# Rearranging the joints of a two-layer decoder step: up phases begun pair by pair, block sums moved, two norm banks, groups held over a phase border

## The chip, the cores and the metric

The kernel runs on all 8 cores of one Trainium2 chip. Each core holds one eighth of the batch (one prompt sequence of 2048 positions and 16 decode tokens, 2064 columns in all) and all weights pass through each core; the cores do not talk to each other. The metric is the device time in microseconds (us) of the slowest core.

The program has a second, slower state. In some executions the cores of one die, sometimes of both, show a lower granted TensorE clock and the whole is some per cent longer: in a run of the kernel before of 1492.06 us the cores of one die took 1473.2 to 1490.5 us at a mean clock of 0.837 to 0.852, those of the other 1317.0 to 1322.5 us at 0.977 to 0.980; both dies were lower in a run of 1513.85 us (0.822 to 0.826 and 0.942 to 0.945).

Engine names: PE is TensorE (matmuls), DVE is VectorE, ACT is ScalarE, POOL or Pool is GpSimd. PEld is the weight load of PE, which overlaps its matmuls (PE is busy 1270.9 and PEld 808.9 us in one span of 1338.7, below).

## The reference, cut to what matters

Layer 0 has a pooling mixer and a gated convolution, layer 1 a chunked gating mixer. Both end in an output projection, a residual addition, an RMSNorm and a SwiGLU feed-forward block.

```python
for layer in range(DEPTH):                       # DEPTH = 2
    h = rmsnorm(x, norm_mix[layer])
    if layer % 2 == 0:
        z = h @ w_in_even[e]                     # the "first projection" below
        ...                                      # pooling windows 2/4/8/16, short convolution
        mix = jnp.concatenate([a_out, b_out], axis=-1) @ w_out_even[e]   # "even out projection"
    else:
        z = jax.nn.gelu(h @ w_in_odd[o], approximate=False)              # "v" and "u" phases
        c_out, v = chunk_gating(z, norm_sg[o], w_s[o], b_s[o])
        mix = c_out @ w_out_odd[o]               # "odd out projection"
    x = x + mix
    h = rmsnorm(x, norm_ffn[layer])
    x = x + swiglu(h, ffn_w_gate[layer], ffn_w_up[layer], ffn_w_down[layer])
return rmsnorm(x, norm_final), ...

def rmsnorm(x, g):
    y = xf * lax.rsqrt(jnp.mean(xf * xf, axis=-1, keepdims=True) + EPS)
    return (y * g).astype(x.dtype)

def swiglu(h, w_gate, w_up, w_down):             # 1024 -> 2816 -> 1024
    return (jax.nn.silu(h @ w_gate) * (h @ w_up)) @ w_down
```

## The kernel before

Activations lie with features on partitions and tokens along the free dimension. The 2064 tokens form 6 tiles of 344 columns, and two neighbouring tiles form a pair. Features form 8 groups of 128.

The feed-forward block is cut into 22 chunks of 128 hidden features. They are taken in three rounds per layer; a round is an *up phase* (gate and up products of 6 or 8 chunks) and a *down phase* (the projection back of these chunks into the residual). An up product of one chunk and one pair of tiles uses the seven-multiplication scheme for a 2x2 block product: 7 x 4 = 28 matmuls of 344 columns instead of 32. The price is block sums: sums of weight blocks (`ssum`, four per chunk, into `S`) and sums of activation blocks (`tsum`, four per pair, into `T`; one of them rewrites a part of `hT` in place).

```python
FFN_GROUPS = ((8, 8, 6), (6, 8, 8))

NB = banks[7]                                   # one PSUM bank for every norm

class Norm:
    POPS = (2, 1, 1, 0, 1, 1, 1, 1)
    def square(self, n, c):                     # squares on ACT, their running sum on Pool
        ...
        act(rng[i][:], xs(c, n), AF.Square)
        dst = accb[a] if c == lastc else acc[a]
        tt("pool", dst[:], acc[a][:], rng[i][:], ALU.add)
    def mid(self, n):                           # sum over partitions on PE, then 1/sqrt on ACT
        for i, p_ in enumerate(ps):
            sc.op("pe", lambda E, i=i, p_=p_: E.matmul(
                NB[:, 0:TW], lhsT=ones[:], rhs=p_[:], start=(i == 0), stop=(i == len(ps) - 1)))
        rsqrt_mean(NB, NB[:, 0:TW])
        self.q += [(n, c) for c in range(KC)]   # eight scalings to do on DVE: hT = x * g * NB
        if self.sums and n % 2:
            self.q += [("T", n // 2, i) for i in range(4)]     # the block sums of the pair
    def before(self, n, m):
        if m == 4 and n > 0:
            self.mid(n - 1)
...
def tsum(p, i):                                 # block sums of the activations
    if i == 0:   tt("dve", T1, b12, b11, ALU.subtract)
    elif i == 1: tt("pool", b12, b22, b12, ALU.subtract)       # rewrites hT
    elif i == 2: tt("dve", T2, b22, T1, ALU.subtract)
    else:        tt("dve", T4, b21, T2, ALU.subtract)
...
def out_proj(l, slots, nm):
    todo = [(c, i) for c in (0, 1) for i in range(4)]
    for n in range(NT):                         # 6 tiles
        for m in range(8):                      # 8 output groups of 128 features
            nm.before(n, m)
            bk = nbank()
            proj(bk, slots[m // 4], (m % 4) * 128, n, mix, 512)   # 8 matmuls
            xacc(bk, m, n)                      # residual addition on DVE
            nm.step(n, m)                       # squares, scalings, block sums
            if n >= 2 and m in (2, 6) and todo:
                ssum(l, *todo.pop(0), eng="pool")              # weight sums on Pool
...
def ffn_up(l, g):
    order = [(c, p) for c in range(c0, c1) for p in range(NPAIR)]
    if g == 0:
        order[0:6] = [(0, 0), (0, 1), (1, 0), (1, 1), (0, 2), (1, 2)]
    ...
    for i in range(len(gs) + 2):                # software pipeline over products cur, prv, pp
        if cur:
            cur.pe(1); cur.pe(7); cur.c1(); cur.c7()
        if pp:
            pp.mb(dst(pp))
        if prv:
            prv.pe(5); prv.pe(2); prv.d1(); prv.ga(); prv.ma(dst(prv))
        if cur:
            cur.pe(6); cur.c2()
            if i == 0 and active and g == 0 and active[0].parts:
                drip(len(active[0].q))
                active[0].mid(NT - 1)           # norm of the last tile, inside the up phase
            cur.pe(4); cur.d2()
        ...
...
def ffn(l, nm, before_last=None):
    for g in range(3):
        ffn_up(l, g)
        ...
        ffn_dn(l, g, nm if g == 2 else None)
...
def n_sq(n, cs=range(KC)):                      # squares of the first projection
    ...
        who = (("act", "dve")[c % 2] if n == 0 else ("act", "dve", "pool")[c % 3] if n < 3 else
               ("act", "act", "pool")[c % 3] if n < 4 else ("act", "pool")[c % 2])
```

Cuts are marked with `...`; some lines were joined or left out. In the profile, `L433`, `L436` and `L430` are the helpers behind every DVE or Pool `tensor_tensor`, every DVE `scalar_tensor_tensor` and every ACT operation, so there one goes by tile names: `xTs` is the residual, `hTs` its normed copy, `tmp` the buffers of the up products, `acc` and `accb` the running sums of squares. `L554` is the norm-sum matmul, `L659` an up product, `L703` a projection, `L809` a down projection, `L901` the pooling part of the first projection.

## Time and profile before

| | before |
|---|---|
| time, median of 6 runs | 1326.03 us (1321.43 to 1444.6) |
| profiled execution, slowest core (core 7, at clock 0.81 for 158.4 us) | 1338.7 us |
| profiled execution, core 2 (undisturbed) | 1319.1 us |
| matmuls | 8200 |

The page of the profile first: busy time and instructions of each engine on the slowest core, then the busy share of PE and the granted clock in 40 equal slices (tenths), then the chain of waits that ended last.

```profile
PE 1270.9 (95%) x8200; PEld 808.9 (60%) x8200; DVE 827.7 (62%) x1621; ACT 539.4 (40%) x1157; POOL 268.6 (20%) x343
...
PE   8799999699999999999889999888999999999996
...
PEclk9988887899999999999999999888999999999999
...
PE 82%; DVE 10%; issue 4%; ACT 2%; POOL 1%; DMA 1%; DVEq 0%; POOLq 0%; ACTq 0%; SPq 0%
```

What PE waits for stands in the view of its waits. This is core 2, before; the columns are the releaser, us in total, times, and the longest wait in us.

```profile
PE bank L554 <- DVE hTs L436: 16.9, 9, 3.7
PE bank L659 <- DVE tmp_107 L433: 12.1, 8, 3.8
PE bank L659 <- ACT bank L430: 9.1, 5, 4.3
PE bank L901 <- DVE hTs L436: 7.9, 3, 4.7
...
PE bank L554 <- POOL accb_92 L433: 3.2, 3, 1.9
```

The first line is the norm-sum matmul. It writes bank 7, and DVE's eight scalings of the tile before still read bank 7. The waits of up products (`L659`) on `tmp_107` and on ACT are DVE and ACT behind in the first products of an up phase.

These lines are PE's timeline on core 2 in the even out projection (start, duration, instruction, count, and in brackets the idle time before it with what ended it).

```profile
190.65 4.83 PE L703 MATMUL bank<-mix,wring_48 128*128 128x344 f16 x32
...
199.16 0.31 PE L554 MATMUL bank<-accb_92,ones 128*128 128x344 bf16 x1 [3.68 <-DVE hTs L436]
199.30 6.50 PE L703 MATMUL bank<-mix,wring_46 128*128 128x344 f16 x32
```

The same 32 matmuls take 4.83 us before a wait of 3.68 us and 6.50 us after it. In the clock record of this core the clock is 1.00 up to 199.71 us, 0.50 for the next 3.41 us, and 1.00 again. The up phase that follows shows the half clock more strongly. These are windows of 3 us on core 2: length, then busy us with instruction counts of PE, PEld, DVE, ACT, POOL, then granted clock, DMA share and GB/s.

```profile
218.00:221.00 3.00, 0.00 (x0) 0.00 (x0) 3.00 (x6) 0.85 (x3) 2.80 (x4) 0.87 0.00 0
221.00:224.00 3.00, 1.30 (x4) 0.44 (x4) 3.00 (x10) 0.88 (x2) 1.50 (x2) 0.50 0.27 31
224.00:227.00 3.00, 1.98 (x8) 1.07 (x9) 0.76 (x2) 0.96 (x2) 1.31 (x2) 0.50 0.34 61
227.00:230.00 3.00, 3.00 (x12) 1.65 (x11) 2.93 (x6) 0.90 (x2) 0.90 (x1) 0.50 0.00 0
```

For the first three of these us PE does nothing, DVE is full and Pool is busy beside it; by the clock record the clock is 0.50 from 220.19 to 230.43 us. At 0.50 matmuls of 344 columns start every 0.286 us (226.69 to 230.13), at full clock every 0.146 (next paragraphs). In the first projection there is another kind of loss. This is core 2's timeline of DVE and Pool there, some lines of it.

```profile
59.52 4.28 DVE L436 SCALAR_TENSOR_TENSOR mix<-P_70,Sg_88 128x344 f16<-128x344 f32 x1
59.79 0.78 POOL L433 TENSOR_TENSOR mix<-P_67 128x344 f16<-128x344 f32 x1
60.51 0.77 POOL L433 TENSOR_TENSOR sq_77<-xTs 128x344 bf16<-128x344 f32 x1
...
62.66 0.75 POOL L433 TENSOR_TENSOR sq_83<-xTs 128x344 bf16<-128x344 f32 x1
```

One pooling instruction of DVE takes 4.28 us while Pool runs a row of its own instructions. In the same trace such an instruction took 0.52 us with Pool idle (at 65.11 us, for one) and 0.81 to 0.82 us beside one or two of Pool's (at 46.09, 49.15 and 73.53 us).

### The profile page before, as it was taken

How to read it: one execution, taken by the hardware profiler on the slowest of the kernel's cores; microseconds unless marked ns; L12 is line 12 of the kernel's file. 1: busy time of each engine (PE TensorE's matmuls, PEld its weight loads, DVE VectorE, ACT ScalarE, POOL GpSimd, SP SyncE). 2: the span in 40 equal slices, each digit the busy share in tenths (PEclk: the TensorE clock that was granted, in tenths of full speed). 3: DMA queues.
4: the chain of work that ended last, by engine and by line, in shares of the span. 5: the costliest groups of instructions: out<-in, count | busy, mean ns of one | idle time of the engine just before them, and what ended most of it. 6: DMA issues, size and time to landing. Idle time of an engine off the chain costs nothing.

```text
span 1338.7 us, 25276 instructions; the slowest of 8 cores (1314.7 to 1338.7 us)
## 1 busy us (share of the span) xinstructions
PE 1270.9 (95%) x8200; PEld 808.9 (60%) x8200; DVE 827.7 (62%) x1621; ACT 539.4 (40%) x1157; POOL 268.6 (20%) x343
## 2 busy tenths in 40 slices
PE   8799999699999999999889999888999999999996
PEld 4466665366666666666544566555666666666664
DVE  3878557856545665455765676885665665456566
ACT  3332333355204550055557434344503551055543
POOL 4300057500000000000641103761000000000054
PEclk9988887899999999999999999888999999999999
DMA  9442230063101620042333103003311421034024
GB/s 240 119 67 33 33 49 1 9 95 64 33 1 33 96 48 16 1 64 33 64 64 63 35 1 49 1 1 65 63 17 33 92 51 18 1 64 79 2 89 167
DMA packets 18913, 68.64 MB, mean 51 GB/s; under 512 B 2928, under 2 KB 3056, under 8 KB 17744
## 3 DMA queue, kind: packets, MB, share of 16 engines
q0 software_dynamic: 13472, 54.99, 23.4%
q1 hardware_dynamic: 4736, 11.26, 2.5%
q8 instruction: 69, 1.13, 0.3%
q10 hardware_dynamic: 576, 0.77, 0.2%
q14 instruction: 60, 0.49, 0.1%
HBM read 105.84 MB, written 9.18 MB: 86 GB/s over the span
## 4 chain that ended last, share of the span: by engine, by line
PE 82%; DVE 10%; issue 4%; ACT 2%; POOL 1%; DMA 1%; DVEq 0%; POOLq 0%; ACTq 0%; SPq 0%
PE bank L659 38%; PE bank L809 18%; PE bank L703 14%; PE bank L1101 4%; PE bank L1067 4%; DVE hTs L436 2%; DVE xTs L433 2%; PE bank L901 2%; DVE mix L433 1%; DVE xTs L436 1%; DMA xTs<-xT 1%; DVE T_98 L433 1%; PE bank L554 1%; PE bank L1114 1%; PE bank L890 1%
## 5 line engine op out<-in xcount | busy, mean ns | idle before, releaser
L433 DVE TENSOR_TENSOR xTs<-bank,xTs 128x344 f32<-128x344 f32 x384 | 197.1, 515 | 169.7 <-PE bank L809 132.4
L809 PE MATMUL bank<-mix,wring_46 128*128 128x344 f16 x1152 | 215.0, 309 | 0.0
L809 PE MATMUL bank<-mix,wring_48 128*128 128x344 f16 x960 | 187.0, 309 | 0.0
L430 ACT ACTIVATE bank<-bank 128x344 f32<-128x344 f32 x161 | 71.2, 442 | 227.6 <-DVE xTs L433 210.3
L809 PEld LDWEIGHTS bank<-mix,wring_46 128*128 128x128 f16 x1152 | 112.5, 98 | 54.9
L809 PEld LDWEIGHTS bank<-mix,wring_48 128*128 128x128 f16 x960 | 93.9, 98 | 46.1
L430 ACT ACTIVATE tmp_111<-bank 128x344 f32<-128x344 f32 x132 | 60.4, 458 | 119.1 <-DVE tmp_108 L433 43.3
L659 PE MATMUL bank<-hTs,raw_102 128*128 128x344 f16 x576 | 103.2, 316 | 0.0
L436 DVE SCALAR_TENSOR_TENSOR hTs<-xTs,vecs_s,bank 128x344 f16<-128x344 f32 x184 | 97.9, 565 | 7.5 <-ACT bank L430 7.1
L430 ACT ACTIVATE tmp_110<-bank 128x344 f32<-128x344 f32 x132 | 60.4, 457 | 100.5 <-DVE tmp_106 L433 31.6
L659 PE MATMUL bank<-hTs,raw_103 128*128 128x344 f16 x504 | 87.6, 310 | 0.0
L659 PE MATMUL bank<-hTs,raw_104 128*128 128x344 f16 x504 | 87.4, 309 | 0.2 <-DVE xTs L433 0.2
L659 PEld LDWEIGHTS bank<-hTs,raw_102 128*128 128x128 f16 x576 | 57.6, 100 | 30.1 <-issue 0.3
L703 PE MATMUL bank<-mix,wring_48 128*128 128x344 f16 x384 | 66.5, 338 | 0.0
L181 POOL DMA_DIRECT2D raw_102<-wts x16 | 8.6, 538 | 286.3 <-DVE tmp_107 L433 166.6
L430 ACT ACTIVATE rng_94<-xTs 128x344 bf16<-128x344 f32 x82 | 40.2, 490 | 63.5 <-DVE xTs L433 56.1
L433 DVE TENSOR_TENSOR mix<-tmp_110,tmp_109 128x344 f16<-128x344 f32 x66 | 38.5, 583 | 44.0 <-ACT tmp_110 L430 44.0
L703 PE MATMUL bank<-mix,wring_46 128*128 128x344 f16 x384 | 65.0, 333 | 0.0
L659 PEld LDWEIGHTS bank<-hTs,raw_103 128*128 128x128 f16 x504 | 49.5, 98 | 24.5
L659 PEld LDWEIGHTS bank<-hTs,raw_104 128*128 128x128 f16 x504 | 49.2, 98 | 24.6 <-issue 0.5
L433 DVE TENSOR_TENSOR mix<-tmp_110,tmp_108 128x344 f16<-128x344 f32 x66 | 34.1, 517 | 47.1 <-ACT tmp_110 L430 47.1
L430 ACT ACTIVATE rng_93<-xTs 128x344 bf16<-128x344 f32 x82 | 40.2, 490 | 57.2 <-DVE xTs L433 54.4
(262 smaller groups left out, 2208.5 us busy)
## 6 DMA issues: line engine op xcount, KB each, us to landing
raw_102<-wts POOLq DMA_DIRECT2D x16, 512.0 KB, 6.2
yT<-xTs SPq DMA_DIRECT2D x22, 344.0 KB, 2.3
raw_103<-wts POOLq DMA_DIRECT2D x14, 512.0 KB, 6.2
raw_104<-wts POOLq DMA_DIRECT2D x14, 512.0 KB, 6.3
xTs<-xT POOLq DMA_DIRECT2D x10, 688.0 KB, 17.4
wring_46<-wts POOLq DMA_DIRECT2D x12, 512.0 KB, 9.2
wring_48<-wts POOLq DMA_DIRECT2D x10, 512.0 KB, 8.4
wring_48<-wts POOLq DMA_DIRECT2D x2, 1024.0 KB, 16.9
```

The costliest lines, as they stand in the source:

```text
L430: return sc.op("act", lambda E: E.activation(out=out, in_=in_, func=func, **k))
L433: return sc.op(eng, lambda E: E.tensor_tensor(out=out, in0=in0, in1=in1, op=op))
L436: return sc.op("dve", lambda E: E.scalar_tensor_tensor(out=out, in0=in0, scalar=scalar, in1=in1, op0=op0, op1=op1))
L554: sc.op("pe", lambda E, i=i, p_=p_: E.matmul(NB[:, 0:TW], lhsT=ones[:], rhs=p_[:], start=(i == 0), stop=(i == len(ps) - 1)))
L659: last = E.matmul(bk[:, 0:TW], lhsT=w_[:, o_ + k * 128:o_ + (k + 1) * 128], rhs=rhs(k), start=(first and k == 0), stop=(k == 3), skip_grou ...
L703: last = E.matmul(bk[:, 0:TW], lhsT=wt[:, o:o + 128], rhs=src[:, k, tok(n)], start=(k == 0), stop=(k == KC - 1))
L809: last = E.matmul(bk[:, 0:TW], lhsT=w_(jl)[:, m * 128:(m + 1) * 128], rhs=mix[:, jl, tok(n)], start=(jl == 0), stop=(jl == n_ - 1))
L890: sc.op("pe", lambda E: E.matmul(bk[:, 0:512], lhsT=ones[:], rhs=spinw[:], start=True, stop=True))
L901: last = E.matmul(pdst[n][g][:, 0:TW], lhsT=wt0[:, k * 512 + g * 128:k * 512 + (g + 1) * 128], rhs=hT[:, k, tok(n)], start=(k == 0), stop= ...
L1067: last = E.matmul(bk[0:ntok, :], lhsT=hT[:, k, t0:t0 + ntok], rhs=wv[:, k * 512:(k + 1) * 512], start=(k == 0), stop=(k == KC - 1))
L1101: last = E.matmul(bu[:, 0:w], lhsT=wt[:, o:o + 128], rhs=hT[:, k, c0:c0 + w], start=(k == 0), stop=(k == KC - 1))
L1114: last = E.matmul(bm[:, q * 128:(q + 1) * 128], lhsT=vN[:, q0 + q, h * 128:(h + 1) * 128], rhs=wsT[:, h * 128:(h + 1) * 128], start=True, ...
```

## The change

The intent is to take the waits of PE out of the joints between phases without changing the mathematics or the number of matmuls:

1. The first five chunks of the first up phase of a layer run pair by pair, so that the phase begins with products of tiles 0 and 1 and reaches tiles 4 and 5 only after ten products. The last norm and the block sums of pairs 1 and 2 move behind these products. Five slots for weights and weight sums replace three.
2. The block sums of pairs 1 and 2 leave the projection phases; the weight sums and the rewriting `tsum` go from Pool to DVE.
3. Norms alternate between two banks, each output group is followed by one scaling, and the norm sum comes one group later.
4. The last group of an out projection or of a down phase is held and issued inside the next up phase; the first group of a down phase is pulled into the end of its up phase.
5. In the first projection the squares of tiles 2 to 5 all go to ACT, and one pooling task runs per tile, interleaved with the convolution; three of the pooling tasks move to the even out projection.
6. The chunks of layer 0 are grouped 6, 8, 8 instead of 8, 8, 6.

```diff
-FFN_GROUPS = ((8, 8, 6), (6, 8, 8))
+FFN_GROUPS = ((6, 8, 8), (6, 8, 8))
...
-        NB = banks[7]
+        def NB(n):
+            return banks[7 if n % 2 else 2]
...
             def step(self, n, m):
                 self.square(n, m)
-                k_ = self.POPS[m]
-                if self.sums and n % 2 and n > 1 and m in (3, 4, 5, 6):
-                    self.pop_sum()
-                self.pop_h(k_)
+                if n < NT - 1 or m < 5 or self.late:
+                    self.pop(1)
 
             def before(self, n, m):
-                if m == 4 and n > 0:
+                if m == 5 and n > 0:
                     self.mid(n - 1)
...
             elif i == 1:
-                tt("pool", b12, b22, b12, ALU.subtract)
+                tt("dve", b12, b22, b12, ALU.subtract)
...
-                    if n >= 2 and m in (2, 6) and todo:
-                        ssum(l, *todo.pop(0), eng="pool")
+                    if (n, m) == (NT - 1, KC - 1):
+                        held.append(lambda bk, n=n, m=m: group(n, m, bk))
+                    else:
+                        group(n, m)
+                    ...
+                    if tasks:
+                        tasks.pop(0)()
+                    elif todo and (n > 0 or m > 3):
+                        ssum(l, *todo.pop(0))
+                    if (n, m) in tsums:
+                        tsum(0, tsums[(n, m)])
...
             if g == 0:
-                order[0:6] = [(0, 0), (0, 1), (1, 0), (1, 1), (0, 2), (1, 2)]
+                order = [(c, p) for p in range(NPAIR) for c in range(5)] + order[15:]
...
+                early = {0: [lambda: nm.pop(4)], 1: [lambda: nm.pop(4)], 2: ss(3), 3: ss(4) + ts(1, 0), 4: ts(1, 1, 2, 3),
+                         5: [lambda: nm.pop(4)], 6: [lambda: nm.pop(4)], 7: ts(2, 0, 1), 8: ts(2, 2, 3)}
...
+                    release(banks[(ctr[0] - len(gs) + 2) % 3 if g else 6])   # the held group
+                    if g == 0 and i == 1:
+                        nm.mid(NT - 1)
...
-                who = (("act", "dve")[c % 2] if n == 0 else ("act", "dve", "pool")[c % 3] if n < 3 else
-                       ("act", "act", "pool")[c % 3] if n < 4 else ("act", "pool")[c % 2])
+                who = ("act", "dve")[c % 2] if n == 0 else ("act", "dve", "pool")[c % 3] if n == 1 else "act"
```

Cuts are marked. Not shown: the new places of buffers (for the five slots and for the split weights of the v phase), SiLU done in place in its PSUM bank, the interleaving of pooling and convolution tasks, and the order of the loads.

## The prediction

> **What bounds it.** TensorE: the page of the slowest core has PE busy 1270.9 of 1338.7 us and 82% of the chain of waits. Cores 6 and 7 ran 75-200 us at clock 0.81 (cores and windows views), the other six did not, so I read core 2 (1319.1 us). [...] the trace shows 0.81, on two cores only. I assume that state stays as rare.

> Dense, core 2 does 174 matmuls of 344 columns in 25 us (0.144 us each). Counts in 5 us windows give the lost time (estimates):
> - first projection, 30-75 us: 249 done of 326: 11 us
> - even out projection and start of its up phase, 185-255: 22 us
> - odd one, 820-900: 20 us
> - last down phase of layer 0, 635-680: 9.5 us
> - six up-to-down transitions: 4.5 us; four back: 1.5 us
> - last down phase, 1260-1310: 3 us; tail about 8 us.
> PE's waits agree: norm-sum matmul on DVE's hTs 16.9 us, up-phase matmuls on DVE tmp_107 12.1 and on ACT 8.4, first projection on hTs 7.9.

> **What the change does.** The matmul count stays.
> 1. Two norm banks, one hTs write per group: the norm-sum matmul no longer waits for eight scalings of 0.56 us.
> 2. Pair-first order: the up phase starts on tiles 0 and 1; the last norm and two of three sets of block sums (1.2 us each) hide under products of 28 matmuls (4.0 us). DVE has 2.1 us of work per product plus 21 us extra over nine: slightly too much, 3 us lost.
> 3. Pool's block work goes to DVE: weight sums (1.15-1.8 us on Pool, 0.415 on DVE), hTs sum (2.8 us on Pool). T_98 took up to 3.34 us beside it. [...] at 59.5 us a pooling instruction took 4.28 us, not 0.82, while Pool ran a subtraction and four squares. Those squares go to ACT.
> 4. One pooling task instead of two per tile in the first projection. Three go to the even out projection, whose DVE work I estimate as 47 x 0.51 + 32 x 0.56 + 12 x 0.42 + 4 x 1.2 + 5.5 = 57 us, against 55 of PE; more where Pool's 0.84 us additions block.
> 5. Held groups and a first down group fill the transitions.
> 6. Layer 0's last down phase gets 8 instead of 6 matmuls per group: 9.2 us per tile against 8.6 of DVE; 6.9 was DVE-bound.

> **On the path.** Gains: first projection 5, even projection and start 12 (10 stay lost), odd 13, layer-0 last down 7, transitions 4, last down 2: 43 us. Cost: three down loads at once may be 1-2 us late, twice: -2. So 1326 - 41, rounded to 1282 us for fewer clock drops (0.77-0.86 in those windows); 8 in 10 within 1262 to 1304. Faster by over 2%: 0.85; within: 0.13; slower: 0.02.

> **Right or wrong by.** PE's wait of norm-sum on hTs near 0; waits on tmp_107 gone; both projections at 33 or more matmuls per 5 us; no Pool operation on hTs; the 4.28 us instruction back to about 0.8; a small wait of the first down group on a DMA.

> **What would break it.** DVE becoming the limit in the even projection or the first nine products; late loads of chunks 3 and 4[...].

Gains of 43 us less 2 make 41, and 1326 - 41 = 1285 was put at 1282 us for fewer clock drops. The -2 for late loads is a guess for which no trace is named. That Pool's additions of 0.84 us "block" DVE can be seen in the trace after the change: in the even out projection five instructions of DVE's weight sums that ran beside such an addition (160 to 168 us) took 0.74 to 1.05 us, the seven later ones, which overlap one by 0.05 us at most, 0.41; the residual additions took 0.48 to 0.51 us, beside Pool's or not.

## More of the kernel before

PE is the bounding engine, but a fifth of the chain is not PE. A "busy" PE also ran at clock 0.50 for 40.2 us of the span (core 2), so its 95% overstates how close it is to its own limit.

All waits of PE on core 2 listed by the view add up to about 63 us.

Last, the out projection and the first up phase of each layer as whole phases, core 2, in the columns of the windows view.

```profile
151.82:215.47 63.65, 59.05 (x391) 38.42 (x389) 49.68 (x93) 27.12 (x59) 46.89 (x50) 0.97 0.16 27
215.47:332.91 117.44, 105.09 (x677) 67.73 (x674) 75.99 (x148) 56.80 (x124) 23.07 (x24) 0.93 0.30 53
```

PE's limit is known from this trace: an undisturbed down phase does 384 matmuls of 344 columns in 56.00 us, 0.1458 us each. So the 672 matmuls of that up phase need 98.0 us, and 117.44 us are 19 too many.

## The result, and the profile after

| | before | after |
|---|---|---|
| time, median | 1326.05 us (20 runs, 1321.43 to 1467.6) | 1251.74 us (10 runs, 1251.36 to 1252.07) |
| ratio of fast runs, 95% interval | | 0.9452 (0.9443 to 0.9462) |
| profiled, core 2 | 1319.1 us | 1249.4 us |
| matmuls | 8200 | 8200 |

The change is 5.5% faster: 74.3 us between the medians. Forecast was 1282 us, within 1262 to 1304, so the direction was right and the time lies below the range. Ratios here and below are the mean time of one kernel's fast runs over that of the kernel before in the same rounds, so they are not quite the ratio of the medians that are quoted. Of the 20 runs before, 7 were above 1341 us (slow state); of the 10 after, none.

The same lines of the page after, again for the slowest core:

```profile
PE 1227.1 (98%) x8200; PEld 796.7 (64%) x8200; DVE 810.5 (65%) x1648; ACT 544.2 (44%) x1176; POOL 209.5 (17%) x302
...
PE   7999999999999999999999999999999999999996
...
PEclk9999999999999999999999999999999999999999
...
PE 95%; DVE 2%; issue 1%; DMA 1%; ACT 1%; DVEq 0%; POOL 0%; SPq 0%; ACTq 0%; POOLq 0%
```

The chain is PE for 95%, the clock is full in every slice, and all eight cores are between 1245.2 and 1250.4 us at a mean clock of 0.995 to 0.997. PE's waits on core 2, after:

```profile
PE bank L875 <- ACT sq_80 L438: 3.4, 1, 3.4
PE bank L941 <- DVE hTs L444: 2.3, 1, 2.3
...
PE bank L563 <- POOL accb_92 L441: 1.5, 1, 1.5
PE bank L650 <- DVE hTs L444: 0.9, 2, 0.5
```

(`L563` is now the norm sum, `L650` the up product, `L694` the projections, `L941` the pooling part of the first projection and `L875` the norm sum there; `L441`, `L444` and `L438` are the helpers.) The waits listed fall from about 63 to about 12 us. The same two phases after, core 2, in the columns of the windows view (this up phase has 18 products of 28 matmuls, 504, and one matmul at its border is counted too):

```profile
147.56:206.44 58.88, 58.06 (x399) 38.77 (x397) 55.23 (x114) 27.74 (x62) 36.75 (x43) 1.00 0.17 29
206.44:280.66 74.22, 73.75 (x505) 49.11 (x506) 53.70 (x111) 41.20 (x92) 5.75 (x11) 1.00 0.33 58
```

Since group sizes differ, phases are compared by *lost time*: duration minus matmuls x 0.1458 us. All on core 2:

| phase | forecast: lost before, gained | lost before | lost after | gained |
|---|---|---|---|---|
| up to the first out projection | 11, 5 | | | 4.3 |
| even out projection and its first up phase | 22, 12 | 26.0 | 1.8 | 24.2 |
| odd out projection and its first up phase | 20, 13 | 23.1 | 1.0 | 22.1 |
| last down phase of layer 0 | 9.5, 7 | 8.3 | 0.0 | 8.3 |
| the four other up phases (transitions) | 6, 4 | 5.3 | 0.0 | 5.3 |
| last down phase | 3, 2 | 5.5 | 1.7 | 3.8 |
| v and u phases | 0 | | | 1.3 |
| late loads | -2 | | | 0 |
| tail | 0 | | | 0 |
| sum | 41 | | | 69.3 |

Core 2's span fell by 69.7 us, so the table is complete to half a microsecond. (For the first row and for v and u the gain is the difference of the durations.) The metric fell by 74.3 us; the rest is the spread of the cores, since in the profiled execution before the six undisturbed cores reached from 1314.7 to 1322.6 us and two were longer still.

Two thirds of the gain sit at the two out projections with the up phases behind them. The same loss can be split by kind. In the six phases before that lose most, PE was busy about 21 us longer than its matmuls need at full clock (2.3 and 6.8 in the even pair of phases, 2.3 and 6.2 in the odd pair, 2.3 and 0.9 in the two last down phases), so at most 21 of their 63 us (26.0 + 23.1 + 8.3 + 5.5) were half clock, and the rest waits. The clock record of the profile gives 17: PE was busy for 34 us at a clock of 0.50 in these phases, and half of that is lost (0.286 us per matmul there, against 0.146). Over the whole execution of core 2 this loss fell from 20.1 to 1.7 us, about 18 of the 69.7 us gained.

The pooling instruction that took 4.28 us takes 0.51 us after (DVE's timeline, core 2, after):

```profile
69.46 0.51 DVE L444 SCALAR_TENSOR_TENSOR mix<-P_70,Sg_88 128x344 f16<-128x344 f32 x1
```

DVE's timeline in the even out projection, core 2, after, will matter below:

```profile
169.82 0.50 DVE L441 TENSOR_TENSOR xTs<-bank,xTs 128x344 f32<-128x344 f32 x1
170.25 0.56 DVE L444 SCALAR_TENSOR_TENSOR hTs<-xTs,vecs_s,bank 128x344 f16<-128x344 f32 x1
170.73 0.41 DVE L441 TENSOR_TENSOR S_100<-raw_105,S_100 128x512 f16<-128x512 f16 x1
171.06 0.50 DVE L441 TENSOR_TENSOR xTs<-bank,xTs 128x344 f32<-128x344 f32 x1
```

The addition lasts 0.50 us but the next instruction starts 0.43 us after it; the scaling lasts 0.56 us and gives way after 0.48; the weight sum lasts 0.41 and gives way after 0.33. The recorded durations of the 113 DVE instructions that start in this phase add up to 63.7 us, more than the 58.88 us that the phase lasts; DVE's busy time, in which an overlap counts once, is 55.23 us. So the durations cannot be what DVE's work costs.

### The profile page after: what moved, and what is told of

It reads as the page before. It is cut to its first block, busy times and chain, and to the rows that moved or that the text cites. A ratio compares the mean times of both kernels' runs of the same rounds, so it can differ in the third digit from the quotient of the medians.

```text
span 1250.4 us, 24992 instructions; the slowest of 8 cores (1245.2 to 1250.4 us)
## 1 busy us (share of the span) xinstructions
PE 1227.1 (98%) x8200; PEld 796.7 (64%) x8200; DVE 810.5 (65%) x1648; ACT 544.2 (44%) x1176; POOL 209.5 (17%) x302
## 4 chain that ended last, share of the span: by engine, by line
PE 95%; DVE 2%; issue 1%; DMA 1%; ACT 1%; DVEq 0%; POOL 0%; SPq 0%; ACTq 0%; POOLq 0%
PE bank L650 43%; PE bank L830 24%; PE bank L694 15%; PE bank L1103 5%; PE bank L1137 4%; PE bank L941 2%; DMA xTs<-xT 1%; PE bank L875 1%; PE bank L930 1%; PE bank L1150 1%; DVE hTs L444 0%; DVE xTs L444 0%; PE bank L563 0%; DVE xTs L441 0%; DVE mix L441 0%
## 5 line engine op out<-in xcount | busy, mean ns | idle before, releaser
L438 ACT ACTIVATE bank<-bank 128x344 f32<-128x344 f32 x425 | 188.3, 443 | 412.0 <-PE bank L650 210.7
L441 DVE TENSOR_TENSOR xTs<-bank,xTs 128x344 f32<-128x344 f32 x384 | 196.3, 512 | 120.8 <-PE bank L830 115.7
L830 PE MATMUL bank<-mix,wring_46 128*128 128x344 f16 x1152 | 215.0, 309 | 0.0
L830 PE MATMUL bank<-mix,wring_48 128*128 128x344 f16 x960 | 187.0, 309 | 0.0
L830 PEld LDWEIGHTS bank<-mix,wring_46 128*128 128x128 f16 x1152 | 112.7, 98 | 55.2
L830 PEld LDWEIGHTS bank<-mix,wring_48 128*128 128x128 f16 x960 | 93.9, 98 | 46.1
L444 DVE SCALAR_TENSOR_TENSOR hTs<-xTs,vecs_s,bank 128x344 f16<-128x344 f32 x184 | 98.3, 563 | 25.0 <-ACT bank L438 22.7
L650 PE MATMUL bank<-hTs,raw_105 128*128 128x344 f16 x504 | 87.2, 309 | 0.0
L650 PE MATMUL bank<-hTs,raw_104 128*128 128x344 f16 x504 | 87.2, 309 | 0.0
L650 PE MATMUL bank<-hTs,raw_106 128*128 128x344 f16 x432 | 74.7, 309 | 0.9 <-DVE hTs L444 0.9
L650 PEld LDWEIGHTS bank<-hTs,raw_105 128*128 128x128 f16 x504 | 49.3, 98 | 24.2
L650 PEld LDWEIGHTS bank<-hTs,raw_104 128*128 128x128 f16 x504 | 49.3, 98 | 24.2
L438 ACT ACTIVATE rng_93<-xTs 128x344 bf16<-128x344 f32 x82 | 40.2, 491 | 49.8 <-DVE xTs L441 44.1
L438 ACT ACTIVATE rng_94<-xTs 128x344 bf16<-128x344 f32 x82 | 40.2, 491 | 49.0 <-DVE xTs L441 41.5
L694 PE MATMUL bank<-mix,wring_48 128*128 128x344 f16 x384 | 59.7, 309 | 0.0
L441 DVE TENSOR_TENSOR mix<-bank,tmp_112 128x344 f16<-128x344 f32 x66 | 34.0, 516 | 38.7 <-ACT bank L438 38.7
L694 PE MATMUL bank<-mix,wring_46 128*128 128x344 f16 x384 | 58.0, 309 | 0.7 <-DVE mix L441 0.7
L650 PEld LDWEIGHTS bank<-hTs,raw_106 128*128 128x128 f16 x432 | 42.1, 98 | 22.1 <-issue 1.6
L441 DVE TENSOR_TENSOR mix<-bank,tmp_113 128x344 f16<-128x344 f32 x66 | 34.0, 516 | 33.5 <-ACT bank L438 33.5
L694 PEld LDWEIGHTS bank<-mix,wring_46 128*128 128x128 f16 x384 | 37.5, 98 | 19.1 <-issue 0.8
L694 PEld LDWEIGHTS bank<-mix,wring_48 128*128 128x128 f16 x384 | 37.6, 98 | 18.4
```

Source lines behind the costliest of these rows:

```text
L438: return sc.op("act", lambda E: E.activation(out=out, in_=in_, func=func, **k))
L441: return sc.op(eng, lambda E: E.tensor_tensor(out=out, in0=in0, in1=in1, op=op))
L444: return sc.op("dve", lambda E: E.scalar_tensor_tensor(out=out, in0=in0, scalar=scalar, in1=in1, op0=op0, op1=op1))
L650: last = E.matmul(bk[:, 0:TW], lhsT=w_[:, o_ + k * 128:o_ + (k + 1) * 128], rhs=rhs(k), start=(first and k == 0), stop=(k == 3), skip_grou ...
L694: last = E.matmul(bk[:, 0:TW], lhsT=wt[:, o:o + 128], rhs=src[:, k, tok(n)], start=(k == 0), stop=(k == KC - 1))
L830: last = E.matmul(bk[:, 0:TW], lhsT=w_(jl)[:, m * 128:(m + 1) * 128], rhs=mix[:, jl, tok(n)], start=(jl == 0), stop=(jl == n_ - 1))
```

## The experiments

The theory (in the expectations: S, with variants) was that PE lost its time to the named waits and to the half clock after them, that each part of the change removes its own wait, and that DVE has enough room because its cost is its start-to-start pace and not the recorded duration. Rivals: DVE's load, counted by recorded durations, was the limit (D); the lengthening of DVE's instructions beside Pool's made the loss (P). A separate question is whether a stall costs only its wait or also a stretch at half clock behind it (C). Differences in us against the kernel after are between medians of different sessions. The median before in the sessions used was 1324.5 to 1327.1 us, so a difference below 2 or 3 us is not resolved that way, and where a small one matters the ratios are compared.

### One bank again (undo)

```diff
         def NB(n):
-            return banks[7 if n % 2 else 2]
+            return banks[7]
...
                     if g == 0 and i == 1:
+                        for f in early.pop(1):
+                            f()
                         nm.mid(NT - 1)
```

(The second edit keeps the order of scalings and norm sum valid with one bank.)

> The changed kernel with a single norm bank. Theory S[...]: each norm-sum matmul then waits for the last scaling of the tile before, about 1.2 us for 5 tiles in 4 phases: 20 to 28 us slower than 1251.7, and the waits of the norm-sum matmul on DVE hTs come back at 15 to 25 us. Theory D (VectorE's load was the limit and the change relieved it): the second bank takes no work from VectorE, so under 6 us slower. Theory P (Pool's block sums beside VectorE were the cost): under 6 us slower.

Measured: 1300.19 us, ratio 0.9805 (0.979 to 0.9821), 48.5 us slower than after. This is twice what the theory expected. PE's waits on core 2 of this run:

```profile
PE bank L563 <- DVE hTs L444: 24.6, 10, 6.4
PE bank L563 <- POOL acc L441: 10.9, 8, 1.4
```

The wait on the scalings is back, for ten norm sums and up to 6.4 us. It is larger than before (16.9). By its code the changed kernel begins the scalings one group later and does one per group, an order that needs the second bank; that this is the reason was not tested. The bank is the largest of the parts that were undone here, but its 48.5 us is the worth of the bank in the new order, not its share of the gain.

### The second bank alone, added to the kernel before

```diff
         def nbank():
+            if nrot[0] == 7:
+                return banks[(0, 1, 3, 4, 5, 6)[nxt("bank6", 6)]]
             return banks[nxt("bank", nrot[0])]
-        NB = banks[7]
+        def NB(n):
+            return banks[7 if n % 2 else 2]
```

> The kernel before with only the second norm bank (its scaling schedule, order and block sums stay). Theory S: the waits of the norm-sum matmul on DVE hTs (16.9 us on core 2) nearly go, and with them two half-clock stretches: 12 to 20 us faster than before. Rival (the bank is worth much only with the scalings spread one per group and the pair order, since the next wait takes over): under 6 us faster.

Measured: the fast runs are 1307.2 and 1307.4 us (two others at 1328 to 1330), ratio 0.9877 (0.9853 to 0.9901), 16.3 us faster than before. The expected size came. PE's waits on core 2:

```profile
PE bank L558 <- POOL accb L435: 14.8, 10, 3.0
PE bank L663 <- DVE tmp L435: 13.9, 10, 3.8
PE bank L663 <- ACT bank L432: 9.3, 6, 4.4
```

The 16.9 us on `hTs` are gone, and in their place the norm sum waits for Pool's running sum of squares, 14.8 us. The waits of the up phase stay. So the bank alone frees one wait and exposes the next. In the full change that one falls to 1.5 us. The emptier Pool has a part in this (with the sums back on Pool, below, the wait returns); the part of the later norm sum (`m == 5`) was not tested.

### The order of chunks undone

```diff
-                order = [(c, p) for p in range(NPAIR) for c in range(5)] + order[15:]
+                order[0:6] = [(0, 0), (0, 1), (1, 0), (1, 1), (0, 2), (1, 2)]
...
-                early = {0: [lambda: nm.pop(4)], 1: [lambda: nm.pop(4)], 2: ss(3), ...
+                early = {0: ts(1, 0, 1, 2, 3) + [lambda: nm.pop(4)], 1: [lambda: nm.pop(4)], 2: [lambda: nm.pop(8)],
+                         3: ts(2, 0, 1, 2, 3), 5: ss(3), 6: ss(4)}
```

> The changed kernel with the old order of the first products (two pairs of tiles at once, then the third) and its norm and block-sum work pulled forward to match. Theory S: the last norm and two sets of block sums are needed within 4 products instead of 10, so 8 to 14 us lost at each of two up-phase starts, 16 to 28 us slower in all, with TensorE's waits on hTs and T. Theory D and P: the same VectorE work, Pool stays out, so 0 to 8 us slower.

Measured: 1269.24 us, ratio 0.9572 (0.9557 to 0.9588), 17.5 us slower than after, inside the theory's range. The two first up phases of a layer take 82.59 and 82.94 us instead of 74.22 and 74.35, together 17.0 us. The pair-first order is worth this because it leaves time for the norm and the block sums before the products that need them.

### Sums on Pool again

```diff
-                tt("dve", b12, b22, b12, ALU.subtract)
+                tt("pool", b12, b22, b12, ALU.subtract)
...
-                        ssum(l, *todo.pop(0))
+                        ssum(l, *todo.pop(0), eng="pool")
```

> The changed kernel with the weight block sums of the projection phases and the block sum that rewrites hTs back on Pool. Theory P: T and pooling instructions stretch to 2 to 4 us again, 10 to 20 us slower. Theory S: some delay of Pool's norm additions, but the two banks and the order leave slack: 2 to 8 us slower. Theory D: VectorE is relieved of about 13 us of work by durations, so 0 to 4 us faster.

Measured: 1264.24 us, ratio 0.9535 (0.9518 to 0.9552), 12.5 us slower. The out projections take 64.57 and 63.55 us instead of 58.88 and 57.97, which is 11.3 of it. The size fits one theory, the mechanism does not: in the out projections DVE was busy for only 49.42 of 64.57 and 42.72 of 63.55 us. What PE waited for, core 2:

```profile
PE bank L563 <- POOL accb L441: 10.0, 4, 3.8
```

Pool's timeline, core 2:

```profile
176.03 1.16 POOL L441 TENSOR_TENSOR raw<-raw 128x512 f16<-128x512 f16 x1
177.15 0.84 POOL L441 TENSOR_TENSOR acc<-acc,rng 128x344 f32<-128x344 f32 x1
```

Its weight sums of 1.15 us stood in front of its additions of squares (0.84 us), the additions came late, and the norm sum waited for them. What PE waited for in this run was Pool's queue, not DVE. In the kernel before DVE also had instructions that took longer beside Pool's (a block sum `T_98` of 3.34 us beside a Pool sum of 2.78 us and an addition, at most 1.24 after); the share of that in the gain was not tested apart.

### Groups of layer 0 as before

```diff
-FFN_GROUPS = ((6, 8, 8), (6, 8, 8))
+FFN_GROUPS = ((8, 8, 6), (6, 8, 8))
...
-                            for q in range(3):
+                            for q in range(4):
                                 dn_load(l, g, q)
```

> The changed kernel with layer 0 split in groups of 8, 8 and 6 chunks again. Theory D as predicted (VectorE costs the durations of its instructions, 0.50 + 0.56 = 1.06 us per group against 0.875 of six matmuls): its last down phase is limited by VectorE, 8 to 9 us slower. Theory S with start-to-start costs (0.43 + 0.48 = 0.91): 1.5 to 3 us slower, and the phase takes about 44 us for 288 matmuls, against 51.0 before.

Measured: 1258.31 us, ratio 0.9488 (0.9473 to 0.9503), 6.6 us slower. The last down phase of layer 0 takes 48.87 us for 288 matmuls, which need 42.0. This lies between the two expectations, and neither named the cause. Pool's timeline in that phase, core 2 (idle before in brackets):

```profile
610.53 0.84 POOL L441 TENSOR_TENSOR acc<-acc,rng 128x344 f32<-128x344 f32 x1 [0.20 <-ACT bank L438]
611.57 0.84 POOL L441 TENSOR_TENSOR acc<-acc,rng 128x344 f32<-128x344 f32 x1 [0.20 <-POOL acc L441]
```

Each addition reads the one before, and they follow each other at 1.04 us. Seven per tile are 7.3 us; the tile's 48 matmuls of PE are 7.0 us. The wait that ends last is the one for Pool: PE's waits in this phase are 6.2 us on Pool's `accb`, five times. But Pool was busy for only 16.77 of 25.00 us (600 to 625 us) and itself waited for squares of ACT, and DVE's two instructions per group at their pace make 8 x 0.91 = 7.3 us per tile as well. Two tiles took 8.6 and 8.25 us. So the round from DVE over ACT and Pool to PE's norm sum and back is longer than PE's work, and no run separates its parts. The prediction had called this phase DVE-bound. With groups of 8, PE has 64 matmuls per tile, 9.3 us, and the round fits.

### Nothing held over a border (undo)

```diff
-                    if (n, m) == (NT - 1, KC - 1):
-                        held.append(lambda bk, n=n, m=m: group(n, m, bk))
-                    else:
-                        group(n, m)
+                    group(n, m)
...
                 def dn_first():
                     if final:
                         act_warm_lnexp()
-                    one()
...
-                while len(todo) > (0 if final else 1):
+                while todo:
```

A first run of this edit, with three others, fell on a chip whose cores all ran at a clock of 0.935 to 0.957 (the kernel before took 1362.85 to 1376.74 us there); those four runs (this one 1310.57 us, ratio 0.9563; the two with useless DVE additions 0.9536 and 0.9662; the squares further down) are not used, and the edits were run again.

> e6_no_hold again for the same reason. Theory S: 6 to 9 us slower than 1251.7 (six up phases of 1.2 to 1.5 us). Rival: 0 to 3 us.

Measured: 1260.28 us, ratio 0.9511 (0.9496 to 0.9525), 8.5 us slower, as expected. PE's waits gain 4.4 us on DVE `tmp` and 2.0 us on `xTs`. Filling the borders was worth about twice the 4 us of the prediction.

### Squares on ACT alone, added to the kernel before

```diff
-                who = (("act", "dve")[c % 2] if n == 0 else ("act", "dve", "pool")[c % 3] if n < 3 else
-                       ("act", "act", "pool")[c % 3] if n < 4 else ("act", "pool")[c % 2])
+                who = ("act", "dve")[c % 2] if n == 0 else ("act", "dve", "pool")[c % 3] if n == 1 else "act"
```

> e5_squares_only again, since its chip ran the kernel before at 1368 us. The kernel before with the squares of tiles 2 to 5 on ACT alone. Theory P: the 4.28 us pooling instruction falls to about 0.8, 3 to 5 us faster than before. Rival: 0 to 1.5 us faster, as VectorE's second pooling task and ACT's row of eight squares bind instead (v1_squares_early gained 5.4 us by moving those squares).

Measured: fast runs 1320.28 to 1321.05 us, ratio 0.9966 (0.9953 to 0.998), 4.5 us faster than before. (On the slow chip the same edit gave a ratio of 0.9979 with an interval of 0.9921 to 1.0037, which decides nothing.) The first out projection starts at 147.06 us instead of 151.82, the same as in the changed kernel (147.56), and PE's wait on `hTs` in the first projection falls from 7.9 to 2.8 us. So this one line is worth the whole gain of the first projection. The pooling instruction of 4.28 us falls to 1.40 us in this run, not to the 0.8 expected; the six such instructions of DVE between 35 and 80 us last 0.76 us on average, against 1.29 before. That Pool's squares no longer run beside DVE is the likely reason (4.28 us beside five of Pool's instructions before, 0.51 us with Pool idle after), but it is not isolated: the edit also takes three squares of tile 2 from DVE.

### What DVE's work costs: useless additions in the out projections

Here additions of a PSUM bank and a residual tile into a spare buffer were put into tiles 2 to 5 of both out projections of the changed kernel: 2 per tile, then 8. The second edit has the condition `True` instead of `m % 4 == 1`.

```diff
                 xacc(bk, m, n)
                 nm.step(n, m)
+                if n >= 2 and m % 4 == 1:
+                    tt("dve", tmp[2 + m % 3][:], bk[:, 0:TW], xs(m, n), ALU.add)
```

> e7_dve_2 again, since its chip ran the kernel before at 1368 us and clock 0.94 to 0.96. Two useless VectorE additions per tile in tiles 2 to 5 of both out projections. By durations 8 us slower than 1251.7; by start-to-start times 0 to 2 us slower.

Measured: 1258.05 us, ratio 0.9503 (0.9484 to 0.9523), 6.3 us slower.

> e8_dve_8 again for the same reason. Eight per tile. By durations 32 us slower than 1251.7; by start-to-start times 15 to 20 us slower.

Measured: 1277.55 us, ratio 0.9651 (0.9628 to 0.9673), 25.8 us slower. Both results fall between the two expectations (durations 8 and 32, start-to-start 0 to 2 and 15 to 20), so these times alone do not decide. Nor does the difference between the two runs: 48 further additions cost 1277.55 - 1258.05 = 19.5 us, 0.41 us each, which is near the start-to-start pace of 0.43. But DVE's spare time took up a part of them, and other waits and half clock came on top: in the second run PE waited 10.5 us for Pool's `accb`, and 64 matmuls after one such wait took 10.95 us instead of 9.50. What decides against the recorded durations is their sum in the trace after the change, 63.7 us in a phase of 58.88. In the first run the odd projection's tiles kept PE's full pace, as this line of PE's timeline of core 2 shows (64 matmuls in 9.50 us, 0.148 us each); of the 1.8 us by which the phase is longer (59.79 against 57.97), 1.6 are one wait on ACT where the up phase begins:

```profile
780.38 9.50 PE L694 MATMUL bank<-mix,wring 128*128 128x344 f16 x64
```

In the even projection DVE was busy 58.31 of 61.66 us with two additions per tile. So the changed kernel stands close to the edge there: it had room for DVE's work, but very little of it.

### What a stall costs: forced waits

In the four later up phases (two of each layer), three times in each and twelve in all, DVE was given useless additions and PE a matmul that waits for the last of them; 5 additions each time in the first run, 9 in the second.

```diff
+                if cur and g and i in (6, 10, 14):
+                    for _ in range(4):                       # 8 in the second run
+                        tt("dve", acc[1][:], xs(0, 0), xs(1, 0), ALU.add)
+                    tt("dve", accb[0][:], xs(0, 0), xs(1, 0), ALU.add)
+                    sc.op("pe", lambda E: E.matmul(banks[7][:, 0:TW], lhsT=ones[:], rhs=accb[0][:], start=True, stop=True))
```

> The changed kernel with 12 forced stalls of TensorE in steady up phases: each a useless matmul that waits for 5 useless VectorE additions, about 2.3 us idle by estimate. Both theories: about 12 x 2.3 + 1.8 = 29 us slower than 1251.7 (24 to 36), granted clock stays at 1.00 in the up phases.

Measured: 1318.33 us, ratio 0.9959 (0.9936 to 0.9983), 66.6 us slower than after. The expectation missed, for the stalls were 3.5 us on average (2.8 to 3.8) instead of 2.3 and the clock fell. (In the stall shown next the five additions start 0.57 us apart, from 344.02 to 346.31 us, after two weight sums that DVE did while PE already stood idle.) This is one stall in PE's timeline of core 2.

```profile
346.96 0.44 PE L775 MATMUL bank<-accb,ones 128*128 128x344 bf16 x1 [3.83 <-DVE accb L441]
```

These are the windows around it, in the columns as above; the clock is the third number from the end.

```profile
344.00:346.00 2.00, 0.00 (x0) 0.00 (x0) 1.69 (x5) 0.00 (x0) 0.00 (x0) 1.00 0.00 0
...
348.00:350.00 2.00, 2.00 (x8) 1.03 (x7) 0.00 (x0) 0.64 (x2) 0.00 (x0) 0.50 0.04 8
350.00:352.00 2.00, 2.00 (x8) 1.03 (x7) 0.52 (x1) 0.26 (x1) 0.00 (x0) 0.50 0.00 0
...
354.00:356.00 2.00, 2.00 (x15) 1.33 (x14) 0.89 (x2) 1.34 (x3) 0.00 (x0) 1.00 0.91 168
```

After 3.83 us of idle PE does 8 matmuls per 2 us at clock 0.50 instead of 15 at 1.00. The four up phases took 64.1 us more (116.90 + 112.64 + 113.86 + 112.69 against 4 x 98.0). The waits account for 42.5 of them and the useless matmuls for 1.75, which leaves 19.9 us of half clock, about 1.7 us per stall.

> As e11_stall_4 with 9 additions, about 4.3 us idle each. Theory C[...]: each stall costs 2 to 4 us more than its wait, 45 to 70 us slower than e11_stall_4, with windows at 0.50 after the stalls. Rival (a stall costs its wait): 21 to 26 us slower than e11_stall_4.

Measured: 1348.61 us, ratio 1.0189 (1.0165 to 1.0213), 96.9 us slower than after. The waits are 72.7 us and the four up phases 95.5 us longer, which leaves 21.0 us of half clock. The step from the first run, 30.3 us, is the step of the waits (30.2). The fast runs alone say the same: 66.6 and 96.9 us less the waits and the matmuls leave about 22 us both times. In this case, then, a stall of 2.8 to 6.7 us costs its own length and on average about 1.7 us besides, no more in the run with the long ones. The expected jump between the two runs did not come because the clock already fell to 0.50 after the shorter stalls.

The length of a stall alone does not decide whether the clock falls. In the two profiles of the kernels before and after, on the 14 cores without a stretch at 0.81, all 124 falls and rises of the clock lie within 5 ns on a grid of 3.413 us (the first 5 and the last 20 us left out), and how much of one such window PE was idle tells them apart. These are two windows of the kernel before on core 2, with a wait of 2.07 us in the first, and two on its core 5, across which a wait of 3.75 us lies (from 885.83 us; columns as above).

```profile
636.62:640.03 3.41, 1.34 (x10) 0.72 (x9) 2.60 (x6) 1.58 (x4) 1.96 (x3) 1.00 0.00 0
640.03:643.45 3.42, 3.42 (x14) 1.77 (x13) 2.09 (x4) 1.72 (x4) 1.76 (x3) 0.50 0.03 7
...
884.13:887.55 3.42, 1.70 (x12) 0.91 (x10) 3.32 (x4) 0.92 (x2) 3.28 (x3) 1.00 0.00 0
887.55:890.96 3.41, 1.38 (x10) 0.98 (x11) 2.62 (x4) 0.15 (x1) 0.98 (x1) 1.00 0.00 0
```

### The waits of the kernel before, filled (inconclusive)

```diff
+        def fill(k_, bk):
+            for _ in range(k_):
+                sc.op("pe", lambda E: E.matmul(bk[:, 0:TW], lhsT=hT[:, 0, 0:128], rhs=hT[:, 0, 0:TW], start=True, stop=True))
```

It was called ahead of four of the waits, with 10 to 20 matmuls each.

> The kernel before, with useless matmuls of 344 columns (18 to 20, 2.6 to 2.9 us) put into TensorE's queue just ahead of four waits that its trace shows in each layer (3.7, 4.3, 2.6 and 3.8 us). The work waited for is not sooner. Theory C ([...]0.50 in the 3 us windows of 221 to 230 and 245 to 251 us): the half-clock stretches of about 6 us per layer go, 6 to 16 us faster than before, with granted clock 0.99 in the start of both up phases. Rival (only the waits cost): 0 to 4 us slower, for fillers that outlast their wait.

Measured: runs from 1330.36 to 1505.94 us, no ratio. The profile of core 2 shows the two first up phases at 117.32 and 89.96 us (117.44 and 90.32 before) with 48 more matmuls in them, 7 us of work at no cost, and the even out projection at 66.65 instead of 63.65 us. In the even out projection the fillers ran at 174.76 us, two tiles before the wait of 3.70 us (at 200.55 us) that they were to fill, so that wait stayed; 18 of the 48 fillers in the up phase came after their wait too. One of the four runs is fast (1330.36 us). Nothing is concluded from this run.

### A version that beats both: squares one tile earlier

PE's largest remaining waits after the change are in the first projection, on a square of ACT and on `hTs`. The squares of tile n + 2 were issued before the rest of tile n's convolution.

```diff
             last = n == NT - 1
-            if not last:
-                n_sq(n + 1)
...
             if not last:
                 n_apply(n + 1, G0)
+                if n + 2 < NT:
+                    n_sq(n + 2)
...
         rest, bk0 = conv_front(0, 0, wc)
-        rest()
         n_sq(2)
+        rest()
...
-        rest()
         n_apply(2, G0)
+        n_sq(3)
+        rest()
```

> The changed kernel with ACT's eight squares of the next tile, and the norm's Ln and Exp of tile 2, put ahead of the first convolution tap in ACT's queue. In the changed kernel the norm-sum matmuls of the first projection run at the pace of the squares (0.38 us apart) and each tile takes 11.4 us for 64 matmuls (9.33). Theory: 1 to 2 us per tile for three tiles, 3 to 6 us faster than 1251.7. Rival (VectorE's hTs scalings bind these tiles): within 1 us.

Measured: 1246.38 us (1245.87 to 1246.89, 4 runs, correct), ratio 0.9417 (0.94 to 0.9433), whose interval does not meet that of the change (0.9443 to 0.9462). By the medians it is 5.4 us faster than the change, by the ratios 0.0035 x 1326 = 4.6 us. The norm-sum matmuls of one tile in PE's timeline, core 2, after the change:

```profile
68.14 0.31 PE L875 MATMUL bank<-sq_76,ones 128*128 128x344 bf16 x1
68.52 0.31 PE L875 MATMUL bank<-sq_77,ones 128*128 128x344 bf16 x1
```

And in this version:

```profile
63.78 1.33 PE L875 MATMUL bank<-sq,ones 128*128 128x344 bf16 x8
```

After the change PE got one square every 0.38 us from ACT; in this version all eight lie ready and follow each other in 1.33 us. The first out projection starts at 141.56 us instead of 147.56.

## Why the prediction was right or wrong, point by point

The direction was right, and most of the waits that the prediction named went. The time was wrong: 74 us came where 44 were forecast.

**The step that failed** is "even projection and start 12 (10 stay lost), odd 13". The runs showed 24.2 and 22.1 us, with 1.8 and 1.0 us staying lost, so this term was mis-sized by 21 us of the 28 by which the itemised sum fell short (69.3 against 41). The prediction gives a reason for about 8 of the 17 us that it left lost (2 in the even projection, 3 at each start); for the other 9 it gives none. Three errors of sizing can be seen in it; how the 21 us divide among them is not shown.

- *DVE's cost was taken from recorded durations.* The prediction wrote 0.51 and 0.56 us per instruction, "57 us, against 55 of PE", and "3 us lost" over the first nine products. The pace is 0.43 and 0.48 us from start to start. That 57 us came near DVE's measured 55.23 in the even projection is luck: a list that was too short met costs that were too high, for the recorded durations there add up to 63.7. In the changed kernel DVE was busy 55.23 of the 58.88 us of the even projection and 50.72 of 57.97 of the odd one, and the up phases that follow lost almost nothing. In the trace each of these instructions overlaps the next by 0.07 to 0.08 us. The prediction did not use this.
- *The half clock after a wait was called "fewer clock drops" and given 3 us of the 44.* By the clock record it was about 17 of the 63 us that the kernel before lost in the six phases that lose most, and 18 of the 69.7 us gained on core 2. The matmuls counted as not done already contain it; the prediction treated it as an extra of 3 us, and not as a part that goes with the waits. The stall experiments show the price apart: about 1.7 us per stall on average.
- *Losses were counted in windows of 5 us.* A matmul that crosses a border of windows is counted in both, and the rate of "0.144 us" was slightly low for the same reason; 0.1458 is right. In the stretch from 185 to 255 us the windows count 333 matmuls where 313 start, so 22 us were read where 24.4 were lost; the rest of the 26.0 lies outside this stretch.

The other terms:

- *First projection, 5:* right, 4.3 us, and 4.5 us from the squares alone. The reason, Pool's instructions beside DVE's (4.28 us for one before, 1.40 in that run), agrees with that run but is not isolated by it.
- *Two norm banks:* right. The bank alone gave 16.3 us, and the wait on `hTs` at the norm sum is gone after the change.
- *Pair-first order:* right in kind; undoing it cost 17.5 us, and the waits on `tmp_107` are gone.
- *Pool's block work to DVE:* the worth was right (12.5 us when undone), but in the run that undid it the reason in the out projections was not that DVE's instructions took longer. Pool's queue delayed the additions of squares (10.0 us of PE's waits).
- *Last down phase of layer 0, 7:* 8.3 us. The prediction's cause was too simple: with groups of 6 back, PE waited last for Pool's running sum (6.2 of the 6.9 us lost), at the end of a round over DVE, ACT and Pool, and DVE at its pace needs 7.3 us per tile, not "8.6".
- *Transitions, 4:* under-sized. 5.3 us went from the four other up phases, and undoing the held groups cost 8.5.
- *Last down, 2:* 3.8 us. The two banks and the later norm sum serve there too.
- *Cost of late loads, -2:* a guess, and wrong, 0. The expected small wait of the first down group on a DMA is not in PE's waits.
- *What would break it:* neither of the two came. DVE came near its limit (busy 55.23 of 58.88 us in the even projection, and the additions there show how near) but stayed under it; and five chunks arrived in time. The denser PE kept its clock: all 10 runs lie within 0.7 us, at a mean clock of 0.995 to 0.998.

The parts cannot be added. Undoing bank, order, Pool sums, groups and held groups, and the worth of the squares, give 48.5 + 17.5 + 12.5 + 6.6 + 8.5 + 4.5 = 98 us, more than the 74 of the whole; the bank's 48.5 us undone against 16.3 us added alone shows why, since each part was arranged for the others. What stays open is why the kernel before fell into the slow state in 7 of 20 runs and the kernel after in none of 10; some variants of the changed kernel had slow runs too (1461.2 us with one bank, 1381.04 with nothing held), so that none in 10 may be chance, and no run was made to settle it.

## What to carry to other kernels

Before calling an engine the next limit, measure its pace from the start of one instruction to the start of the next; a sum of recorded durations was here about a sixth too high (0.51 against 0.43 us, 0.56 against 0.48), and in one phase it came out longer than the phase itself. Count a stall of PE as its length plus the half clock that may follow it (here when PE was idle for about 2 of the 3.41 us of one window), and read lost time as duration minus matmuls times the dense rate, not as "PE not busy". When one wait is taken away, ask what stands ready to end last next: here a second bank alone changed a wait on DVE into one on Pool of nearly the same length, and only the other parts of the change made the gain whole.
